# Binary cross-entropy on 67 million elements: the last 49152 elements are moved by eight-row transfers on SyncE

## The chip, the cores and the metric

The kernel runs on one core of a Trainium2 chip. The metric is the device time of one execution in microseconds; lower is better. Single executions of one kernel differ by 1 to 2 us here, so medians of several are quoted, and kernels that are compared ran on the same chip in the same session. All executions were of one state (fast), at a granted clock of 1.00.

## The reference

```
pred:   8192 x 8192, fp32, uniform in 0.01 .. 0.99
target: 8192 x 8192, fp32, 0 or 1
pred = clip(pred, 1e-7, 1 - 1e-7)
out  = -(target * log(pred) + (1 - target) * log(1 - pred))
```

Each element is independent. As target is 0 or 1, out = -ln|pred + target - 1|.

## The kernel before

The flat arrays are cut into chunks of 128 rows; the big ones have 15360 columns. Pred and target each have a ring in SBUF with two big places and one small one. A chunk is loaded by GpSimd (target is cast to bf16 on the way), goes through VectorE (clip; add target - 1), ScalarE (Abs, Ln) and VectorE (times -1), and is stored. The last four chunks are called z (big), a and b (half, 7680 columns) and c (2048 columns). The loads of a, b and c are queued together once a place is free, and these three are stored from SyncE.

```
def store(k):
    queue = nc.sync if k >= n - 3 else nc.gpsimd
    queue.dma_start(out=chunk(out, k), in_=spot(ring_p, k))
...
z, a, b, c = range(n - 4, n)
front(z, (0, 2))       # clip, add, Abs, Ln on the first half
front(z, (1, 2))
back(z, (0, 2))        # times -1
front(a)
back(z, (1, 2))
store(z)
front(b, (0, 2))
front(b, (1, 2))
back(a)
store(a)
front(c)
back(b)
store(b)
back(c)
store(c)
```

Of the kernel before, what the change touches and what calls it, by code (L numbers as in the profile page):

```python
# [1 line left out]

# [4 lines left out]

EPS = 1e-7





BIG = 15 * 1024
HALF = BIG // 2


def plan(total):

    n, last = divmod(total, BIG)  # L20
    assert n > 4 and 0 < last <= 2048
    spots = [(HALF, 0), (HALF, HALF)]
    spots += [(BIG, k % 2 * BIG) for k in range(1, n - 1)]
    end = (n - 1) % 2 * BIG
    return spots + [(HALF, end), (HALF, end + HALF), (last, 2 * BIG)]



@with_exitstack
def kernel(  # L30
    ctx: ExitStack,
    tc: tile.TileContext,
    pred: bass.AP,
    target: bass.AP,
    out: bass.AP,
):






    nc = tc.nc
    fp32 = mybir.dt.float32
    bf16 = mybir.dt.bfloat16
    Alu = mybir.AluOpType
    Act = mybir.ActivationFunctionType
    P = nc.NUM_PARTITIONS

    R, C = pred.shape  # L50
    spots = plan(R * C // P)
    n = len(spots)
    widths = [w for w, _ in spots]
    cols = [sum(widths[:k]) for k in range(n)]

    def chunk(ap, k):
        flat = ap.rearrange("r c -> (r c)")
        return flat[cols[k] * P : (cols[k] + widths[k]) * P].rearrange("(p w) -> p w", p=P)

    pool = ctx.enter_context(tc.tile_pool(name="rings", bufs=1))  # L60
    ring = [P, 2 * BIG + widths[-1]]
    ring_p = pool.tile(ring, fp32, name="ring_p", tag="ring_p")
    ring_t = pool.tile(ring, bf16, name="ring_t", tag="ring_t")
    warm = pool.tile([1, 8], fp32, name="warm", tag="warm")

    def spot(ring, k, part=(0, 1)):
        w, c = spots[k]
        i, m = part
        return ring[:, c + i * w // m : c + (i + 1) * w // m]

    def load(k):
        queue = nc.sync if k == 0 else nc.gpsimd
        nc.gpsimd.dma_start(out=spot(ring_t, k), in_=chunk(target, k))  # L73
        queue.dma_start(out=spot(ring_p, k), in_=chunk(pred, k))  # L74

    def store(k):
        queue = nc.sync if k >= n - 3 else nc.gpsimd
        queue.dma_start(out=chunk(out, k), in_=spot(ring_p, k))  # L78

    def front(k, *part):  # L80
        p, t = spot(ring_p, k, *part), spot(ring_t, k, *part)
        nc.vector.tensor_scalar(  # L82
            out=p, in0=p, scalar1=EPS, scalar2=1 - EPS, op0=Alu.max, op1=Alu.min
        )
        nc.vector.scalar_tensor_tensor(  # L85
            out=p, in0=t, scalar=1.0, in1=p, op0=Alu.subtract, op1=Alu.add
        )
        nc.scalar.activation(out=p, in_=p, func=Act.Abs)  # L88
        nc.scalar.activation(out=p, in_=p, func=Act.Ln)  # L89

    def back(k, *part):
        p = spot(ring_p, k, *part)
        nc.vector.tensor_scalar(out=p, in0=p, scalar1=-1.0, scalar2=None, op0=Alu.mult)  # L93

    with tc.manual_schedule():
        nc.vector.memset(warm, 1.0)  # L96
        for k in range(3):
            load(k)
        nc.scalar.activation(out=warm, in_=warm, func=Act.Ln)  # L99
        front(0)  # L100
        front(1)
        back(0)
        store(0)
        back(1)
        store(1)
        load(3)
        for k in range(2, n - 4):
            front(k, (0, 2))
            front(k, (1, 2))
            back(k, (0, 2))  # L110
            back(k, (1, 2))
            store(k)

            for j in range(k + 2, n if k == n - 5 else k + 3):
                load(j)
        z, a, b, c = range(n - 4, n)
        front(z, (0, 2))
        front(z, (1, 2))
        back(z, (0, 2))
        front(a)  # L120
        back(z, (1, 2))
# [5 lines that stand above are left out]
        front(c)  # L127
        back(b)
        store(b)
        back(c)  # L130
        store(c)


# [1 line left out]
_INS = ['pred', 'target']  # L135
_OUTS = [((8192, 8192), 'float32')]


# [23 lines left out]
```

## Time and profile before

| | before |
|---|---|
| time, median (range) | 1866.58 us (1866.01 to 1866.96), 3 runs |
| span of the profiled run | 1864.1 us |
| VectorE / ScalarE busy | 60% / 48% |
| DMA queues, share of 16 engines | 98.5% + 1.7% |
| last pred loads of chunks a and b land | 1801.4, 1819.6 us |
| compute ends; last landing | 1845.9; 1863.2 us |

How to read it: sixteen DMA engines share every 128-row transfer (each has sixteen completion records) and are busy all the time (98.5% + 1.7%), so what counts is engine time. Every packet has a start and a duration in the trace; of the rows of 7680 fp32 columns of pred in a and b (30720 B) every one takes 1138 to 1151 ns here, so a longer one says that something else took its time. A transfer's completion records, one per engine, show how far the engines have drifted apart: here the last comes within 1.0 us of the first in the first 60 us of the kernel, and 4.0 us after it from 660 us on. Lines from the timeline (start, length, engine, line, operation; in brackets the idle time before it and what ended that):

```profile
1801.49 4.16 DVE L82 TENSOR_SCALAR ring_p<-ring_p 128x7680 f32<-128x7680 f32 x1 [6.53 <-DMA ring_p<-in_pred_dram]
...
1819.62 2.16 DVE L82 TENSOR_SCALAR ring_p<-ring_p 128x3840 f32<-128x3840 f32 x1 [1.70 <-DMA ring_p<-in_pred_dram]
...
1836.33 9.94 SPq L78 DMA_DIRECT2D out_dram<-ring_p  x3
```

VectorE starts on a at 1801.49 and on b at 1819.62, each time just after its pred load has landed on the slowest engine. The stores of a, b and c follow from there.

### The profile page before, as it was taken

How to read it: one execution, taken by the hardware profiler on the slowest of the kernel's cores; microseconds unless marked ns; L12 is line 12 of the kernel's file. 1: busy time of each engine (PE TensorE's matmuls, PEld its weight loads, DVE VectorE, ACT ScalarE, POOL GpSimd, SP SyncE). 2: the span in 40 equal slices, each digit the busy share in tenths (PEclk: the TensorE clock that was granted, in tenths of full speed). 3: DMA queues.
4: the chain of work that ended last, by engine and by line, in shares of the span. 5: the costliest groups of instructions: out<-in, count | busy, mean ns of one | idle time of the engine just before them, and what ended most of it. 6: DMA issues, size and time to landing. Idle time of an engine off the chain costs nothing.

```text
span 1864.1 us, 619 instructions
## 1 busy us (share of the span) xinstructions
DVE 1122.2 (60%) x210; ACT 899.9 (48%) x142; POOL 57.5 (3%) x111
## 2 busy tenths in 40 slices
DVE  4655766555576655557665555766555576655585
ACT  3345553335555333555533355553335555333565
POOL 0000000000000000000000000000000000000000
DMA  9999999999999999999999999999999999999999
GB/s 295 374 357 341 353 343 368 383 384 351 347 352 344 371 382 384 348 349 353 347 367 384 382 352 347 353 345 368 385 382 352 345 353 348 365 387 380 353 334 389
DMA packets 15988, 671.13 MB, mean 360 GB/s; under 512 B 1776, under 2 KB 1776, under 8 KB 1904
## 3 DMA queue, kind: packets, MB, share of 16 engines
q0 software_dynamic: 15408, 658.25, 98.5%
q1 hardware_dynamic: 576, 12.85, 1.7%
q14 instruction: 4, 0.03, 0.0%
HBM read 536.87 MB, written 268.44 MB: 432 GB/s over the span
## 4 chain that ended last, share of the span: by engine, by line
DMA 35%; issue 26%; ACT 22%; DVE 15%; POOL 1%; DVEq 0%; POOLq 0%; PEldq 0%
DMA ring_p<-in_pred_dram 32%; ACT ring_p L88 11%; ACT ring_p L89 11%; DVE ring_p L85 7%; DVE ring_p L82 4%; DVE ring_p L93 4%; DMA out_dram<-ring_p 3%; POOL ring_t L73 0%; POOL out_dram L78 0%; DVEq L157 0%; POOL ring_p L74 0%; POOLq L78 0%; POOLq L73 0%; DVEq L82 0%; PEldq L157 0%
## 5 line engine op out<-in xcount | busy, mean ns | idle before, releaser
L88 ACT ACTIVATE ring_p<-ring_p 128x7680 f32<-128x7680 f32 (+1 forms) x70 | 450.6, 6437 | 941.4 <-DVE ring_p L85 941.4
L85 DVE SCALAR_TENSOR_TENSOR ring_p<-ring_t,ring_p 128x7680 f32<-128x7680 bf16 (+1 forms) x70 | 557.2, 7960 | 2.4
L82 DVE TENSOR_SCALAR ring_p<-ring_p 128x7680 f32<-128x7680 f32 (+1 forms) x70 | 284.0, 4057 | 399.0 <-DMA ring_p<-in_pred_dram 399.0
L93 DVE TENSOR_SCALAR ring_p<-ring_p 128x7680 f32<-128x7680 f32 (+1 forms) x69 | 284.0, 4117 | 321.5 <-ACT ring_p L89 321.5
L89 ACT ACTIVATE ring_p<-ring_p 128x7680 f32<-128x7680 f32 (+1 forms) x70 | 451.1, 6444 | 2.2
L74 POOL DMA_DIRECT2D ring_p<-in_pred_dram x36 | 19.3, 535 | 909.2 <-DMA out_dram<-ring_p 909.2
L78 POOL DMA_DIRECT2D out_dram<-ring_p x34 | 18.2, 537 | 851.0 <-DVE ring_p L93 851.0
L73 POOL DMA_DIRECT2D ring_t<-in_target_dram x37 | 20.3, 550 | 0.8 <-PEq L157 0.8
L99 ACT ACT_TABLE_LOAD x1 | 1.3, 1283 | 0.7 <-PEq L146 0.7
L96 DVE MEMSET warm<- 1x8 f32 x1 | 0.1, 65 | 0.8 <-PEq L146 0.8
L99 ACT ACTIVATE warm<-warm 1x8 f32<-1x8 f32 x1 | 0.2, 208 | 0.0
L146 POOL MEMSET const-float32-0.0<- 128x1 f32 x1 | 0.1, 98 | 0.2 <-issue 0.2
L146 POOL MEMSET const-bfloat16-1.0<- 128x1 bf16 x1 | 0.1, 101 | 0.0
L146 POOL MEMSET const-uint8-127<- 128x1 uint8 x1 | 0.1, 99 | 0.0
L146 POOL MEMSET const-float32-1.0<- 128x1 f32 x1 | 0.1, 98 | 0.0
## 6 DMA issues: line engine op xcount, KB each, us to landing
ring_p<-in_pred_dram POOLq DMA_DIRECT2D x32, 7680.0 KB, 35.9
out_dram<-ring_p POOLq DMA_DIRECT2D x32, 7680.0 KB, 29.2
ring_t<-in_target_dram POOLq DMA_DIRECT2D x32, 3840.0 KB, 46.8
ring_p<-in_pred_dram POOLq DMA_DIRECT2D x3, 3840.0 KB, 34.9
ring_t<-in_target_dram POOLq DMA_DIRECT2D x4, 1920.0 KB, 27.7
out_dram<-ring_p POOLq DMA_DIRECT2D x2, 3840.0 KB, 27.6
out_dram<-ring_p SPq DMA_DIRECT2D x2, 3840.0 KB, 15.7
ring_p<-in_pred_dram SPq DMA_DIRECT2D x1, 3840.0 KB, 18.8
```

Source lines behind the costliest of these rows:

```text
L73: nc.gpsimd.dma_start(out=spot(ring_t, k), in_=chunk(target, k))
L74: queue.dma_start(out=spot(ring_p, k), in_=chunk(pred, k))
L78: queue.dma_start(out=chunk(out, k), in_=spot(ring_p, k))
L82: nc.vector.tensor_scalar(out=p, in0=p, scalar1=EPS, scalar2=1 - EPS, op0=Alu.max, op1=Alu.min)
L85: nc.vector.scalar_tensor_tensor(out=p, in0=t, scalar=1.0, in1=p, op0=Alu.subtract, op1=Alu.add)
L88: nc.scalar.activation(out=p, in_=p, func=Act.Abs)
L89: nc.scalar.activation(out=p, in_=p, func=Act.Ln)
L93: nc.vector.tensor_scalar(out=p, in0=p, scalar1=-1.0, scalar2=None, op0=Alu.mult)
L96: nc.vector.memset(warm, 1.0)
L99: nc.scalar.activation(out=warm, in_=warm, func=Act.Ln)
L146: nc = _bacc.Bacc("TRN2", target_bir_lowering=False, num_devices=1)
```

## The change

Its intent is read from the code, as no text came with it: the tail of the kernel is uneven over the sixteen DMA engines, and an eight-row transfer uses only eight of them (in the profile after, each has eight late completion records, against sixteen for 128 rows). Work taken from the last chunk c (2048 to 1664 columns) is given to these eight. The small chunk's loads are held back by two memsets until the last chunks' loads are queued, and go out ahead of the last stores; its own stores come last.

```
+EIGHT, GROUPS, NARROW = 8, 4, 1536
 ...
+    few_p = pool.tile([GROUPS * EIGHT, NARROW], fp32, ...)
+    few_t = pool.tile([GROUPS * EIGHT, NARROW], fp32, ...)
 ...
+    def move_few(to, of):
+        for g in range(0, GROUPS * EIGHT, EIGHT):
+            nc.sync.dma_start(out=to[g : g + EIGHT], in_=of[g : g + EIGHT])
 ...
         front(z, (0, 2))
         front(z, (1, 2))
+        nc.vector.memset(few_p, 0.0)
+        nc.vector.memset(few_t, 0.0)
+        move_few(few_t, few(target))
+        move_few(few_p, few(pred))
         back(z, (0, 2))
 ...
         store(b)
+        first_pass(few_p, few_t)
         back(c)
         store(c)
+        last_pass(few_p)
+        move_few(few(out), few_p)
```

More of the change, by code (lines that the diff above doesn't have):

```diff
@@ L15, with plan @@
 HALF = BIG // 2
-def plan(total):
-    n, last = divmod(total, BIG)
+EIGHT, GROUPS, NARROW = 8, 4, 1536
+def plan(total, P):
+    n, last = divmod(total - GROUPS * EIGHT * NARROW, BIG * P)
+    last //= P
     assert n > 4 and 0 < last <= 2048
@@ L24, in plan @@
     end = (n - 1) % 2 * BIG
-    return spots + [(HALF, end), (HALF, end + HALF), (last, 2 * BIG)]
+    spots += [(HALF, end), (HALF, end + HALF), (last, 2 * BIG)]
+    assert sum(w for w, _ in spots) * P + GROUPS * EIGHT * NARROW == total
+    return spots
 @with_exitstack
@@ L50 @@
     R, C = pred.shape
-    spots = plan(R * C // P)
+    spots = plan(R * C, P)
     n = len(spots)
@@ L63 @@
     ring_t = pool.tile(ring, bf16, name="ring_t", tag="ring_t")
+    few_p = pool.tile([GROUPS * EIGHT, NARROW], fp32, name="few_p", tag="few_p")
+    few_t = pool.tile([GROUPS * EIGHT, NARROW], fp32, name="few_t", tag="few_t")
     warm = pool.tile([1, 8], fp32, name="warm", tag="warm")
@@ L78, in store, with few, first_pass @@
         queue.dma_start(out=chunk(out, k), in_=spot(ring_p, k))
-    def front(k, *part):
-        p, t = spot(ring_p, k, *part), spot(ring_t, k, *part)
+    def move_few(to, of):
+        for g in range(0, GROUPS * EIGHT, EIGHT):
+            nc.sync.dma_start(out=to[g : g + EIGHT], in_=of[g : g + EIGHT])
+    def few(ap):
+        flat = ap.rearrange("r c -> (r c)")[sum(widths) * P :]
+        return flat.rearrange("(p w) -> p w", w=NARROW)
+    def first_pass(p, t):
         nc.vector.tensor_scalar(
@@ L89, in front, with last_pass @@
         nc.scalar.activation(out=p, in_=p, func=Act.Ln)
+    def front(k, *part):
+        first_pass(spot(ring_p, k, *part), spot(ring_t, k, *part))
+    def last_pass(p):
+        nc.vector.tensor_scalar(out=p, in0=p, scalar1=-1.0, scalar2=None, op0=Alu.mult)
     def back(k, *part):
-        p = spot(ring_p, k, *part)
-        nc.vector.tensor_scalar(out=p, in0=p, scalar1=-1.0, scalar2=None, op0=Alu.mult)
+        last_pass(spot(ring_p, k, *part))
     with tc.manual_schedule():
```

## The prediction

Passages are cut, at the marks, that rest on rules no trace or run of this case shows: which engines a transfer with few rows takes, what a place in SBUF costs, how long a memset takes, and the like. The sum ran as follows. Eight engines carry one small row of each transfer and get 2.91 - 1.36 = 1.55 us more; the other eight get 1.36 us less. If the four trailing engines are all among the other eight, they end at 3.03 - 1.36 = 1.67 us and the eight at 1.9 to 2.55 (0.35 to 1.0, plus 1.55): a gain of 0.5 to 1.1 us. The first rival: if one of the last pair is among the eight, it ends 1.55 us later, and the kernel at 1868.1. The second rival had the small transfers slow each other, and the big ones, by the place in SBUF where they land; the upper part of "+1 to +5" was its estimate.

> **What bounds the kernel now.** I read the page's engine shares first, then the queue table, then the issue table, then busy time by stretch, and last the chain of the final stretch.
>
> ```profile
> span 1864.1 us, 619 instructions
> DVE 1122.2 (60%) x210; ACT 899.9 (48%) x142; POOL 57.5 (3%) x111
> ...
> DMA  9999999999999999999999999999999999999999
> ...
> q0 software_dynamic: 15408, 658.25, 98.5%
> q1 hardware_dynamic: 576, 12.85, 1.7%
> ...
> HBM read 536.87 MB, written 268.44 MB: 432 GB/s over the span
> ```
>
> No compute engine is busy for more than 60% of the span. The two DMA queues together take 98.5% + 1.7%, about 100% of sixteen engines' time, and all forty slices of the DMA row are 9. So the sixteen DMA engines set the time: the span is their work, plus some 2 us before the first packet, plus whatever is uneven at the end. The bytes can't change (the reference reads two and writes one 268 MB array), so only the two ends are left to improve. The end, by stretch (columns: stretch, length, DVE, ACT and POOL busy, clock, share of the DMA engines busy, GB/s):
>
> ```profile
> 1845.50:1855.00 9.50, 0.41 (x1) 0.00 (x0) 0.00 (x0) 1.00 0.98 424
> 1855.00:1859.00 4.00, 0.00 (x0) 0.00 (x0) 0.00 (x0) 1.00 0.96 413
> ...
> 1859.50:1860.00 0.50, 0.00 (x0) 0.00 (x0) 0.00 (x0) 1.00 0.74 311
> 1860.00:1860.50 0.50, 0.00 (x0) 0.00 (x0) 0.00 (x0) 1.00 0.32 131
> 1860.50:1861.00 0.50, 0.00 (x0) 0.00 (x0) 0.00 (x0) 1.00 0.23 98
> 1861.00:1861.50 0.50, 0.00 (x0) 0.00 (x0) 0.00 (x0) 1.00 0.31 131
> 1861.50:1862.00 0.50, 0.00 (x0) 0.00 (x0) 0.00 (x0) 1.00 0.20 82
> 1862.00:1862.50 0.50, 0.00 (x0) 0.00 (x0) 0.00 (x0) 1.00 0.04 16
> ```
>
> Compute is over at 1845.9; for another 17 us the engines drain stores. They are full until 1859.5 and then the share falls in steps: after 1860.0 about a quarter of the engines (four of sixteen) still work, and in the last micro-second 0.04, less than one. The completion records of the last store in the trace say the same more sharply: one increment per engine, after the first (at 1860.18) by 0, 0.03, 0.07, 0.22, 0.23, 0.27, 0.30, 0.32, 0.33, 0.35, 0.54, 1.00 and then 1.95, 2.14, 2.39, 3.03 us. Twelve engines end together, four trail. The mean is 0.82, so a perfectly even end would be at most 3.03 - 0.82 = 2.2 us earlier. That is the whole prize: 0.12% of the time. The trail is no matter of the last store alone: earlier in the run the loads land with a spread of 4.0 us too, the trailing four being some 3.0 to 4.0 behind.
>
> The chain confirms that nothing else is at stake at the end:
>
> ```profile
> 1837.18 3.41 ACT ring_p L89
> 1840.59 0.02 issue
> 1840.62 4.16 DVE ring_p L93
> 1844.77 1.14 DVEq L157
> ```
>
> It leaves DVE at 1844.8 although the span is 1864.1: what follows is queued transfer. The last store took 17.3 us to land for 1024 KB (the issue table), nearly all of it queueing.
>
> [...]
>
> **The change, part by part.** Its sense, as I read it: take work from all sixteen engines and give it to eight, to even out the trail.
>
> *Taken away.* The last chunk goes from 2048 to 1664 columns, 384 fewer. Each engine carries 8 of the 128 rows. From the packet records: a row of the last chunk of 8192 B (pred or out) takes 309 ns, one of 30720 B 1138 ns, so 829 ns for 22528 B, or 0.0368 ns per byte. A target row of 2048 columns (read as fp32, landing as bf16) takes 324 ns, and one of 7680 columns 1152, 0.147 ns per column. So 384 columns fewer save 1536 x 0.0368 = 56.5 ns on pred, the same on out, and 384 x 0.147 = 56.5 on target: 3 x 8 x 56.5 = 1.36 us on every engine.
>
> *Added.* Twelve small transfers (four for each of target, pred, out) of 8 rows x 6144 B[...]: 6144 x 0.0368 + 7.5 = 234 ns, so 12 x 234 = 2.81 us, plus twelve completions of 9 ns (the 4-byte packets) = 0.1. [...] The totals differ only by 0.1 us: work is moved, not removed. (Targets keep their fp32 form in the small chunk[...] and cost as many engine nanoseconds.)
>
> *Waits and engines beside it.* Two memsets of 32 x 1536 on VectorE, [...]run from 1789.8, where VectorE waited 1.0 us for ScalarE and has nothing after 1795.0 until the load that lands at 1801.4. [...] The small loads go out at about 1792 and run between the big packets; they are needed only around 1845. Nothing waits. At the end VectorE gets three small passes and ScalarE two: scaled from the 2048-column rows (1.22, 2.29, 1.90 us) by 0.75, they are 0.91 + 1.72 on VectorE, 1.42 + 1.43 on ScalarE, 0.91 on VectorE. The store of the last chunk then goes out near 1848.5 instead of 1845.9, and the small stores from 1851.4 to 1853. The store in front of them ends on the first engine at 1857.7 - so they join a queue with 4 us of backlog, and no engine runs dry. Cost of compute on the path: 0.
>
> *The sum.* [...] That the shift of 1.36 to 1.55 is so close to half of the trail, (3.03 - 0.3) / 2 = 1.37, makes me believe that the change was sized to exactly this picture.
>
> **The rivals.** First, *the trailing engines are elsewhere*: the records don't tell which engine made which increment. [...] For it: the trail comes as 1.95/2.14 and 2.39/3.03, pairs that could be one in each half. Against it: the fit of the size. [...] Third, *a hidden wait*: the small stores come last on the queue and depend on a chain VectorE, ScalarE, VectorE; if that chain were 4 us later than I have it, the end would show engines dry. I see no wait that long. Fourth, *nothing*: the trail drifts by itself; then the time stays at 1866.6.
>
> **Range and chances.** I give the planned outcome (-0.5 to -1.1) a weight of 0.55, nothing to 0.5 us either way 0.15, and the two loss cases together 0.3 (+1 to +5). The median of these is near -0.6: 1866.58 - 0.6 = 1866.0. Eight times in ten between 1865.0 and 1869.8. Every case is within 0.3% of before, far from 2%: within 2% 0.98, faster 0.01, slower 0.01.
>
> **What would show it.** Right: the DMA share after 1859 stays near 1 longer and falls at once, a spread of the last landings under 2.6 us; the small loads have eight increments late[...]; packets of 6144 B take about 234 ns; VectorE's 6.5 us of idle time before the load that lands at 1801.4 is partly eaten and nothing after moves. Wrong: [...]the tail with half the engines busy for 2 us or longer[...], a front of the last half chunk that starts later than 1819.6 (the small loads hold up the big ones), or a DMA share under 0.9 between 1845 and 1859 (a wait).

## The result, and the profile after

| | before | after |
|---|---|---|
| time, median (range), 6 runs each | 1866.65 us (1865.93 to 1866.96) | 1867.97 us (1866.95 to 1868.35) |
| span of the profiled run | 1864.1 us | 1866.2 us |

The ratio is 1.0007, with a 95% interval of 0.9994 to 1.002. It is the mean time of one kernel's fast runs over that of the other's of the same rounds, so not quite the ratio of the medians. The class is "same". In microseconds the change is slower, by 1.3 at the medians, where a gain of 0.6 had been forecast. Two later sessions gave +1.1 and +0.9, so the sign is no accident.

The page of the kernel after, first lines of its first and third part:

```profile
span 1866.2 us, 649 instructions
DVE 1127.5 (60%) x215; ACT 902.4 (48%) x144; POOL 57.6 (3%) x111
...
q0 software_dynamic: 15408, 657.96, 98.4%
q1 hardware_dynamic: 768, 13.24, 1.7%
```

Still about 100% of sixteen engines. SyncE's queue (q1) has 192 packets more: 96 small rows and 96 semaphore writes. The timeline of the kernel after, at the same places as above:

```profile
1790.52 1.34 DVE L142 MEMSET few_p<- 32x1536 f32 x1 [0.26 <-issue]
...
1792.13 1.34 DVE L143 MEMSET few_t<- 32x1536 f32 x1 [0.27 <-issue]
...
1793.49 1.33 SPq L92 DMA_DIRECT2D few_t<-in_target_dram  x4
1794.87 1.31 SPq L92 DMA_DIRECT2D few_p<-in_pred_dram  x4
...
1802.88 4.16 DVE L99 TENSOR_SCALAR ring_p<-ring_p 128x7680 f32<-128x7680 f32 x1 [5.40 <-DMA ring_p<-in_pred_dram]
...
1822.25 2.16 DVE L99 TENSOR_SCALAR ring_p<-ring_p 128x3840 f32<-128x3840 f32 x1 [2.95 <-DMA ring_p<-in_pred_dram]
...
1838.97 11.37 SPq L88 DMA_DIRECT2D out_dram<-ring_p  x3
```

Read the last three lines against those of before: a starts 1.4 us later, b 2.6 us later, and the store of a goes out 2.6 us later. About 0.45 us of this was there already when target's part of a landed (1792.75 against 1792.29), before any small packet. The rest was lost while the small loads ran, from 1796.8 to 1814.7. The prediction had named exactly this sign: "a front of the last half chunk that starts later than 1819.6". And the tail of the kernel after, by stretch (columns as in the prediction; a packet counts whole in the stretch in which it starts, so the 0.45 at 1859.0 only follows a share of 1.04 from 1855 to 1859):

```profile
1859.00:1859.50 0.50, 0.00 (x0) 0.00 (x0) 0.00 (x0) 1.00 0.45 189
...
1860.50:1861.00 0.50, 0.00 (x0) 0.00 (x0) 0.00 (x0) 1.00 0.81 341
...
1862.00:1862.50 0.50, 0.00 (x0) 0.00 (x0) 0.00 (x0) 1.00 0.68 278
1862.50:1863.00 0.50, 0.00 (x0) 0.00 (x0) 0.00 (x0) 1.00 0.47 190
1863.00:1863.50 0.50, 0.00 (x0) 0.00 (x0) 0.00 (x0) 1.00 0.07 27
1863.50:1864.00 0.50, 0.00 (x0) 0.00 (x0) 0.00 (x0) 1.00 0.06 27
1864.00:1864.50 0.50, 0.00 (x0) 0.00 (x0) 0.00 (x0) 1.00 0.09 37
1864.50:1865.00 0.50, 0.00 (x0) 0.00 (x0) 0.00 (x0) 1.00 0.03 12
```

Most engines now work until 1862.5 to 1863.0, 2.5 us longer than before, and one works alone for the last 2 us. The completion records name that one's half: the last small store's eight increments come at 1863.13 plus 0, 0.13, 0.21, 0.24, 0.26, 0.27, 0.27 and then 2.17 us. So it is among the eight that carry the small rows. All four small stores show this spacing (first to last 2.16, 2.16, 2.17 and 2.17 us), so the same eight carry all four. The last engine of the other eight ends at 1863.5.

The packet records say where the time went. The small packets mostly behave: 55 of the 64 loads take 234 to 247 ns, nine take 271 to 581. The big ones do not. Of the 256 rows of pred in a and b, 75 take longer than their 1138 ns, up to 1951; summed over all of them the excess is 17.0 us, over sixteen engines 1.06 us each. In the kernel before this sum is 0 in the same stretch. It has two clusters, at 1797 to 1801 and at 1809.5 to 1815: while pred's parts of a and b are loaded. Between them, while mostly target's part of b is loaded, small packets start as well (30 of the 64, from 1801 to 1809), yet the pred rows that start there lose 0.07 us. Target rows lose 0.24 us in all, four of them, at 1798 to 1799. And all engines are hit: at 1815.0 sixteen rows of pred are under way, one per engine, and every one of them is stretched, by 69 to 427 ns.

The mean landing over all sixteen engines agrees. From target's part of a to pred's part of c it takes 32.17 us before and 33.39 after. The small loads add 8 x 0.245 us on half the engines, so 0.98 on the mean, and the smaller c takes away 0.90. That leaves 1.14 us lost on the mean. The excess of the pred rows is 1.06 of it; the nine stretched small loads (1.0 us in sum) and the four target rows are the rest.

### The profile page after: what moved, and what is told of

The parts are those of the page before. It is cut to its first block, busy times and chain, and to the rows that moved or that the text cites. A ratio compares the mean times of both kernels' runs of the same rounds, so it can differ in the third digit from the quotient of the medians.

```text
span 1866.2 us, 649 instructions
## 1 busy us (share of the span) xinstructions
DVE 1127.5 (60%) x215; ACT 902.4 (48%) x144; POOL 57.6 (3%) x111
## 4 chain that ended last, share of the span: by engine, by line
DMA 36%; issue 26%; ACT 22%; DVE 15%; POOL 1%; POOLq 0%; DVEq 0%; PEldq 0%
DMA ring_p<-in_pred_dram 33%; ACT ring_p L106 11%; ACT ring_p L105 11%; DVE ring_p L102 7%; DVE ring_p L99 4%; DVE ring_p L112 4%; DMA out_dram<-ring_p 3%; POOL ring_t L83 1%; POOL out_dram L88 0%; DVE few_p L102 0%; ACT few_p L105 0%; ACT few_p L106 0%; POOL ring_p L84 0%; DVE few_p L99 0%; DVE few_p L112 0%
## 6 DMA issues: line engine op xcount, KB each, us to landing
out_dram<-ring_p POOLq DMA_DIRECT2D x32, 7680.0 KB, 29.2
```

## The experiments

"Excess" is, in each profile, the sum over the pred rows of 30720 B (those over 1160 ns) of what they took beyond 1138 ns. Times are medians, with the kernel before of the same session behind; each kernel had 5 timed runs, the kernel before 9 in each session. (When the experiments ran, one pred row each of a_again and all32, of 2212 and 2227 ns, had been left out of the sum; that is the 15.0 in an expectation below, in place of 16.1.)

| run | in short | excess, us | time, us | before, us |
|---|---|---|---|---|
| a_again | the change | 16.1 | 1866.92 | 1865.85 |
| seven | seven rows at a time | 11.9 | 1866.94 | 1865.85 |
| four | four rows of 768 at a time | 2.6 | 1867.42 | 1865.85 |
| all32 | 32 rows in one transfer | 14.9 | 1867.29 | 1865.85 |
| own_port | every fourth row | 0 | 1865.43 | 1865.69 |
| early | small loads earlier | 29.2 | 1867.54 | 1865.69 |
| wide128 | 128 rows of 384 | 0 | 1866.52 | 1865.69 |
| probe | 16 rows of 128 | 0 | 1866.30 | 1865.69 |
| next_port | every fourth row, four partitions down | 8.6 | 1866.86 | 1865.95 |
| own_again | as own_port | 0 | 1865.38 | 1865.95 |
| a_third | the change | 17.7 | 1866.88 | 1865.95 |
| wide_again | as wide128 | 0 | 1866.61 | 1865.95 |

All were correct. No pair is apart by the 95% interval of the ratios, which is about 0.0025 wide here; the verdicts below rest on the packets, and on runs that repeat or don't overlap.

**First session: is it the tilt?** The first theory (L) was the prediction's first rival: the last engine is among the eight that carry the small rows, so the tilt makes it later. The rivals were D (late loads make late stores, and engines run dry) and noise.

The change again, without an edit.

> The changed kernel once more, beside the kernel before on the same chip. Theory L (one of the four trailing engines, the very last, is among the eight that carry the small rows, so it ends 2.9 - 1.36 = 1.55 us later): +1.0 to +1.8 us, the last landing again on the small stores, seven of the eight engines landing together and one 2.2 us behind. Rival D (the small loads delay the big ones, so the last big stores go out late and engines run dry for about 1 us): the same time. Rival N (noise): within 0.3 us of before.

Measured: +1.1 us at the medians. The last landing is on the small stores, one engine 2.1 us behind the first, but the seven others are spread over 1.3 us, not together. L and D both allow it; noise is out.

```
-EIGHT, GROUPS, NARROW = 8, 4, 1536
+EIGHT, GROUPS, NARROW = 7, 4, 1536
```

> Seven rows at a time instead of eight (28 x 1536, the chunk in front 1712 wide)[...]. Each engine is relieved of 336 columns, 1.19 us. [...] Rival D: seven eighths of the delay, about +1.2 us.

Measured: +1.1 us. The trace shows seven increments per small store. L's figures were -0.5 to -1.1 us if the engine now free of small rows was the last, and +1.5 to +1.9 if the last was among the seven. The gain did not come; the other half is missed too, by 0.4. That the seven are among the former eight was my assumption; no trace names the engines. D's figure fits.

```
-EIGHT, GROUPS, NARROW = 8, 4, 1536
+EIGHT, GROUPS, NARROW = 4, 8, 768
```

> Four rows of 768 columns at a time, eight groups (the chunk in front 1856 wide)[...]: 24 packets of about 120 ns = 2.9 us, less the 0.68 us that every engine is relieved of. [...] Rival D: half the bytes in the small loads on half the engines, but just as long a delay on each, +1 us.

Measured: +1.6 us, between the figures of L (+2.2 us if the last engine is among the four that carry the small rows here, -0.3 to -0.6 if not) and D. The trace shows four late increments per small store. It told nothing apart when it ran. Its excess is small, 2.6 us, so its loss has another source; of the four engines, two end 1.5 to 1.7 us after the others, and the tilt of 2.2 us fell on these as well. That is a reading, not a test. The edit also brought a wait that the others don't have: the eighth small store goes out only after the store of c has landed (1863.47), its packets start at 1863.80, and the last landing (1864.59) is on it. By the spacing of the seven before it, this cost about 0.1 us (an estimate).

```
-        for g in range(0, GROUPS * EIGHT, EIGHT):
-            nc.sync.dma_start(out=to[g : g + EIGHT], in_=of[g : g + EIGHT])
+        nc.sync.dma_start(out=to, in_=of)
```

> All 32 rows in one transfer, so all sixteen engines carry two rows each: the same bytes, memsets, extra passes and order, without the tilt towards eight engines. Theory L: no tilt, so 0 to +0.2 us against before. Rival D: the loads are still ahead of the big ones on every engine, half as long: +0.5 to +0.8 us.

Measured: +1.4 us. This fells L as the whole story: all sixteen engines carry small rows (32 rows and sixteen completion records per transfer: q1 has 720 packets against 576), there is no tilt, and the loss is as large. It is also larger than D expected. Looking for what these four share, I found the stretched pred rows, 14.9 us of them here. D has a part in this run as well: the first engine is through with the loads at 1820.54 and with the store of z 20.25 us later, against 18.16 us before, so it stood dry for 2.1 us, because a's pred load came late (1804.3) and with it the store; the mean over the engines from loads to store grew by 0.5 us. In the change itself the same step takes 18.26 us, and the share of busy engines from 1835 to 1845, where the store of a is due, averages 0.93 before and 0.91 after: no dry stretch worth its loss.

**Second session: which partitions?** The new theory, P, took up the prediction's second rival: what costs is the partitions of SBUF that the small loads write. In the change each small load writes eight neighbouring partitions; the edit below spreads the eight rows. My picture of why this should matter was not shown by any trace; the labels own_port and next_port, and "own-port kernel" for the every-fourth-row form, serve as names only. Rival Q: taking turns between two queues is what costs. Rival F: a fixed cost of more transfers.

```
-        for g in range(0, GROUPS * EIGHT, EIGHT):
-            nc.sync.dma_start(out=to[g : g + EIGHT], in_=of[g : g + EIGHT])
+        for g in range(GROUPS):
+            nc.sync.dma_start(out=to[g::GROUPS], in_=of[g::GROUPS])
```

> The change as it is, but each transfer of eight rows takes every fourth row (partitions g, g+4, ... g+28) instead of eight neighbours[...]. Theory P[...]: the big packets of pred keep their 1138 ns (sum of the excess near 0 us against 17.0 and 15.0 us in the two profiles of the change), the mean end of the engines comes 1 us earlier, the time is 0.6 to 1.2 us below the change's, so about 0 to +0.7 against before. Theory L (the tilt alone): the same time as the change, +1.0 to +1.5. Rival Q (taking turns between the two queues is what costs): the excess stays at 15 us.

Measured: 1865.43 us, 0.3 us below before and so better than P's figure, and the excess is exactly 0: every one of the 64 small loads takes 234 or 247 ns and no pred row is stretched. Same bytes, order and waits, and as many packets (768 on q1); what differs is which partitions a transfer writes together, and with it which rows of DRAM go together in it (next_port below settles that it is the partitions). Rival Q is out, and so is L. The timeline of this kernel, to be read against the two above:

```profile
1801.73 4.16 DVE L99 TENSOR_SCALAR ring_p<-ring_p 128x7680 f32<-128x7680 f32 x1 [4.48 <-DMA ring_p<-in_pred_dram]
...
1819.87 2.16 DVE L99 TENSOR_SCALAR ring_p<-ring_p 128x3840 f32<-128x3840 f32 x1 [1.71 <-DMA ring_p<-in_pred_dram]
...
1836.58 12.36 SPq L88 DMA_DIRECT2D out_dram<-ring_p  x3
```

b starts at 1819.87, as before the change (1819.62), though half the engines carry eight more packets by then. And its tail by stretch:

```profile
1860.00:1860.50 0.50, 0.00 (x0) 0.00 (x0) 0.00 (x0) 1.00 0.62 254
1860.50:1861.00 0.50, 0.00 (x0) 0.00 (x0) 0.00 (x0) 1.00 0.44 179
1861.00:1861.50 0.50, 0.00 (x0) 0.00 (x0) 0.00 (x0) 1.00 0.19 77
1861.50:1862.00 0.50, 0.00 (x0) 0.00 (x0) 0.00 (x0) 1.00 0.09 37
1862.00:1862.50 0.50, 0.00 (x0) 0.00 (x0) 0.00 (x0) 1.00 0.03 12
1862.50:1863.00 0.50, 0.00 (x0) 0.00 (x0) 0.00 (x0) 1.00 0.00 0
```

More engines work until 1861 than before (0.62 and 0.44 against 0.32 and 0.23 in the same stretches), fewer after: what the tilt was meant to do. It is not even yet: two of the eight end 1.4 and 1.8 us after the first.

```
         front(z, (0, 2))
+        (the two memsets and the small loads)
         front(z, (1, 2))
-        (the two memsets and the small loads)
```

> The memsets and the small loads one half chunk earlier (between the two halves of the last big chunk's first pass), so that they run while a store and then a target load are in flight, and not beside loads of pred[...]. Theory P: excess of the big packets under 4 us in sum, time 0.6 to 1.2 us below the change's. Theory L: +1.0 to +1.5 as before. Rival Q: excess of about 15 us, now on the packets of other transfers.

Measured: +1.9 us, and the excess is 29.2 us, the largest of all. My expectation was wrong about the place: the small packets come out between big ones, and the eight per engine are spread over 19 us, from 1784.8 to about 1804 (in the change over 18 us, 1796.8 to 1814.7). They started beside a target load, but most ran beside pred's part of a, and none in the free stretch of target's part of b. Read that way it speaks for P, as more small packets beside pred rows make more excess; it did not test what it was made for. The first engine stands dry ahead of the store of z here too, by 1.8 us.

```
-EIGHT, GROUPS, NARROW = 8, 4, 1536
+EIGHT, GROUPS, NARROW = 128, 1, 384
```

> The small chunk as 128 rows of 384 columns, one transfer each: the same bytes and order, all sixteen engines[...], no tilt[...]. Theory P: no excess, time 0 to +0.4 us against before. Rival Q: 16 packets per engine beside the big loads instead of 8 on half of them, so +1 us or more. Rival F (a fixed cost of more transfers, passes and waits at the end): +1 us.

Measured: excess 0, +0.8 us at the medians. There are 256 small load packets, sixteen per engine, and they cost nothing but their own time: from target's part of a to pred's part of c the mean landing takes 32.35 us against 32.17. So Q is out again. The +0.8 is above P's figure.

```
-EIGHT, GROUPS, NARROW = 8, 4, 1536
+EIGHT, GROUPS, NARROW = 16, 1, 128
...
-        move_few(few(out), few_p)
+        to, g = few(out), 0
+        for rows in (8, 4, 2, 2):
+            nc.sync.dma_start(out=to[g : g + rows], in_=few_p[g : g + rows])
+            g += rows
```

> Nearly nothing moved: a small chunk of 16 rows by 128 columns, loaded by one transfer each and stored by 8, 4, 2 and 2 rows[...]. Theories P, L, Q: 0 to +0.3 us against before. Rival F: +1 us. [...]

Measured: +0.6 us at the medians. The increments: the store of c ends on the sixteen engines at 1860.52 plus 0 to 0.37 (ten of them), 1.03, 1.24, 1.76, 2.64, 3.48 and 3.82 us. The eight-row store behind it ends on all of its eight engines between 1860.84 and 1861.94. So the four that trail (1862.28 and later) are all among the other eight in this run: the picture for which the change looks sized. Two of the store's eight are about 1 us behind the other six. L, for which the last of all is among the eight, is contradicted for this run, if an eight-row store takes the same eight engines here as in the change (assumed).

**Third session: the partitions or the crowd, and the change beside its mended form.**

```
-    few_p = pool.tile([GROUPS * EIGHT, NARROW], ...)     # few_t likewise
+    few_p = pool.tile([4 + GROUPS * EIGHT, NARROW], ...)
...
-        move_few(few_t, few(target))                      # few_p and out likewise
+        move_few(few_t[4:], few(target))
```

(from the kernel of own_port)

> The kernel with every fourth row, its small tiles moved down by four partitions (4 to 35)[...]. Theory P:[...] the excess of the big packets is back, 8 to 15 us in sum, and the time 0.7 to 1.3 us above the own-port kernel's. Rival C[...]: excess under 3 us and the time of the own-port kernel.

Rival C: it is the crowd, eight neighbouring rows in one load, that costs.

Measured: the excess is back, 8.6 us, and the time is 1.5 us above own_again's. The rows of DRAM are grouped as in own_port, so it is the partitions that cost. No two rows of a load are neighbours here either, so a crowd isn't needed. Of the 64 small loads, 28 start while at least eight engines are on rows of pred and 46 while any is; at 234 ns each that is 6.6 to 10.8 us (an estimate from these counts), so an exchange of one for one would fit the sum. The change itself has twice the excess (16.1 to 17.7 us), so eight neighbours at once seem to make it worse: both P and C hold a part. From target's part of a to pred's part of c the mean landing takes 32.82 us against 32.23 in own_again; this 0.59 us is the excess over sixteen engines, and the rest of the 1.5 us is not explained (the five runs range over 2.1 us).

The loss is not confined to a few engines: at 1815.0 in the change all sixteen pred rows under way are stretched, and at 1813.0 here all fifteen. So what is shown is that small rows in some partitions slow the pred rows of all engines, and in others (own_port, own_again) of none; through what, no run here shows.

> The own-port kernel again, on the same chip as the change and the kernel without tilt. Expected: excess 0, 0.9 to 1.6 us below the change, -0.6 to +0.2 us against before.

No edit. Measured: 1865.38 us, 0.6 below before, excess 0.

> The change a third time, beside its variants on one chip: +0.8 to +1.5 us against before, excess of the big packets 14 to 18 us in sum, the last landing on the small stores[...].

No edit. Measured: 1866.88, +0.9, excess 17.7; the last landing is again on the small stores. Over all sessions the 16 runs of the change lie between 1866.38 and 1868.35 and the 10 of its every-fourth-row form between 1864.54 and 1865.93: no overlap, and 1.5 us between the medians of the last group.

> No tilt[...] (128 rows by 384) again: if the tilt as such is worth what the prediction said, 0.5 to 1.1 us, this one lies that much above the own-port kernel, so +0.3 to +0.9 against before; excess 0. If the tilt is worth nothing, the two are within 0.3 us.

No edit. Measured: 1866.61, +0.7 us. With the same bytes and an excess of 0 in both, own_port lies 1.1 and 1.2 us below wide128 at the medians of the two sessions. Some 0.2 us of it is engine time, as wide128 has more and smaller packets (an estimate from the packet times); the tilt is worth the rest, about 1 us.

The three parts, then, at the medians: the tilt with its fewer packets about -1.1 us (own_port against wide128); eight neighbouring rows per load instead of every fourth about +1.5 (the change against its every-fourth-row form), of which the packets show 1.1; and +0.6 to +0.8 for having the small chunk at all (wide, probe), of which the traces of wide128 account for some 0.3 as engine time (24 packets of 65 to 78 ns, 1.65 us, against 1.36 saved). The rest of this third part is not explained. In the profiles of wide128, wide_again and probe the engines are 4.3, 4.9 and 5.1 us apart even ahead of the small loads, against 4.0 before, so a wider drift is a candidate; a single profile each, and runs of before that range over 2 us, don't settle it.

The every-fourth-row form beats both kernels at the medians in both of its sessions, against before by 0.3 and 0.6 us, 0.03%; the interval of the ratio (0.9982 to 1.0009) holds 1, so against before this is likely, not shown.

## Why the prediction was right or wrong

The range (1865.0 to 1869.8) and the class held; the forecast within it had the sign wrong. By its own steps:

- **The bound** was right: DMA engine time, with only the tail to win.
- **"Taken away"** was right: rows of c of 1664 columns take 253 ns.
- **"Added"** is the step that failed. The packet's own time was right (234 ns forecast, 234 and 247 measured), but the sum stopped there, at 1.36 us less for the engines without small rows. In the change the small loads beside pred rows also stretch these rows (75 of 256). The missing term measured 17.0, 16.1 and 17.7 us, about 1 us for each of sixteen engines on the mean, and 0 once each load took every fourth row (own_port, own_again).
- **"Nothing waits"** was right for the compute engines: the memsets, 1.34 us each, moved the negation behind them from 1790.80 to 1793.39, and 5.40 us of idle time were still left before a's first pass. It was wrong for the big loads, which landed up to 2.6 us late at b.
- **The tilt's gain** of 0.5 to 1.1 us held about, but only against wide128 (1.1 and 1.2, some 0.2 of it packet time). Against the kernel before, the every-fourth-row form gains 0.3 and 0.6. The change itself did not show the tilt because the stretched rows took more than that.
- **The second rival** (above) named the right place, the partitions that the small loads write, but I gave it part of a weight of 0.3, and its working was not what happened. It had the small loads themselves stretched well beyond their own time; 55 of 64 kept to 234 to 247 ns, and the time was lost on the big rows. The stores, which it had slowed as well, took their 234 ns packets one after the other without stretching (31 of 32, one took 242): seven engines read 6144 B each every 0.24 us, about 179 GB/s in sum.
- **The first rival** gave the best number, 1868.1, and its sign as well, the last landing among the eight. It is still not the cause: without a tilt the loss stayed (all32), with the tilt and every fourth row it went (own_port), and the probe had the trailing four in the other half. A number that fits is not a mechanism.

## What to carry to other kernels

When a small load runs beside big ones, try which partitions it writes: here loads of eight rows stretched the big rows by 16 to 18 us in sum as neighbours (the change), by 8.6 with every fourth row from partition 4 on, and by 0 with every fourth row from partition 0 on; a free stride in the slice decided it. When engines are full, count for each small transfer not only its own packets but what it takes from others, and look for it in the durations of the neighbours' packets, not in its own. The small loads of the change were nearly free beside the load that casts to bf16 (0.24 us of its rows' time) and dear beside the fp32 one (17.0). A queue whose small packets come out between big ones spreads them, here eight per engine over 18 to 19 us, so work out when they really run.
